# A hybrid streaming encoder step on one core: regrouped retention products, sample tile padded to 128, tables and warm-up products moved

## The chip, the core and the metric

The kernel is one launch on one NeuronCore of a Trainium2 chip. The metric is the device time of one execution in microseconds (us), the median of several runs; beside it stands one profiled execution, whose trace is read below. The engines are TensorE (PE in the profile: matrix products into PSUM banks, with its weight loads as PEld), VectorE (DVE), ScalarE (ACT), GpSimd (POOL) and SyncE (SP, which here only issues DMAs). A DMA can be issued by POOL's queue as well.

## What is computed

One inference step of a two-layer trunk for 512 prompt tokens and 64 sample tokens, width 1024, all in float32. Layer 0 runs an mLSTM (4 heads of 128) and a multi-scale retention (4 heads, keys 64, values 128) side by side from one input projection; layer 1 is a latent attention (MLA, 8 heads) with a block-causal mask of chunks of 64. A SwiGLU FFN follows each, and a layer norm follows each part. The three recurrent parts that the change touches, cut from the reference:

```python
# retention, chunk by chunk
a = jnp.einsum('bhtd,bhsd->bhts', qc, kc) * intra
o = jnp.einsum('bhts,bhsv->bhtv', a, vc) + q_dec[..., None] * jnp.einsum('bhtd,bhdv->bhtv', qc, S)
S_new = s_dec[:, None, None] * S + jnp.einsum('bhsd,bhsv->bhdv', kc * k_dec[..., None], vc)
...
# mLSTM, chunk by chunk (stabilised gates in d_mat, m_t, w_inter, w_k, decay)
s = jnp.einsum('bhtd,bhsd->bhts', qc, kc) * jnp.exp(d_mat - m_t[..., None])
num = w_inter[..., None] * jnp.einsum('bhvd,bhtd->bhtv', C, qc) + jnp.einsum('bhts,bhsv->bhtv', s, vc)
C_new = decay[..., None, None] * C + jnp.einsum('bhsv,bhsd->bhvd', vc * w_k[..., None], kc)
...
# MLA, per block of queries
p = jax.nn.softmax(jnp.where(vis, s, -jnp.inf), axis=-1)
return jnp.einsum('bqhk,bkhv->bqhv', p, v)
```

## The kernel before

Tokens stand in five tiles: tile 0 is the 64 sample tokens, tiles 1 to 4 are 128 prompt tokens each. All weights stream from memory in blocks of 512 KB into three raw buffers (`raw0` to `raw2`), issued by SP in the order of their use; each half of a block is split into a high part (a rounding by ACT, line 364) and a low part (a subtraction by DVE, line 362), and a product is three products high x high, high x low, low x high. A product on TensorE is the helper `mm` (line 465), a transpose the helper `transpose` (line 533). An f32 product shows as two records in the trace.

The order of every engine's instructions is fixed when the program is written: the code runs the projections unit by unit, and after each unit a small planner (`tick`) lets background tasks go on whose due time has come on its own clock. Retention, mLSTM and attention are such tasks, so their small products lie between the k steps of the projections. What stands on an engine's queue is worked off in that order, and an instruction that waits holds all behind it. PSUM has eight banks in three pools, each used in a ring: `mm` with three (projections), `x` with four (small products), `o` with one (only used in layer 1 before the change).

At the start, SP brings the input (first half of each row, in pieces) and the weights by turns. POOL's own queue brings the small tables: at lines 587 to 590 the gate weights `wg`, the `rope`, `mask`, `cst` and `ident` tables and the gate bias `bif`; at lines 640 to 649 the selection tables, the initial states `c0` (into `CxS`) and `s0` (into `S[0]`) and the norm vectors. The first projection `rqrk` loops over k, and for each k over tiles 1 and 2, since the weights only just arrive; its second half of the input comes inside the loop, after k = 3 and k = 4. Then come `gate_mm`, `rqrk` for tiles 0, 3 and 4, and `rv` and `mv`. Every `rqrk` tile goes through `ev_qk`: three DVE ops read the bank (lines 706 to 708), three POOL ops add and scale (709, 711, 713), and then TensorE transposes the result into `qkT`.

`retention` has three steps per tile. `s1` makes the four heads' scores, k and q of 64 rows each, in two x banks, and DVE applies the mask into `P` (line 925). `s2` computes for each head in turn the state's increment `up` (64 columns of weights), P times v (128 rows) and q times the state (64 rows); then DVE adds `up` to the state and scales it (lines 944, 947) and does the head norm from the banks (lines 952 to 958). `s3` transposes the result. `mlstm` has the same for one head at a time: `s1` a transpose and two products, `s2` P v, the state's increment and q C; tile 0 has 64 rows in all of these. In layer 1 `sa`, `sb` and `sc` are the scores, the transposes of the probabilities and the product with v; for tile 0 `sc` is nine products of 64 columns into the o bank. `wgp`, `T0`, `T1`, `Z`, `r7` and the like are names of long-lived buffers in SBUF.

Of the kernel before, what the change touches and what calls it, by code (L numbers as in the profile page):

```python
# [8 lines left out]
F32 = mybir.dt.float32  # L9
# [208 lines left out]
class Kern:  # L218
# [335 lines left out]
    def setup(self):  # L554
# [24 lines left out]
        wg = self.T0[:, 4300:4364]  # L579
# [43 lines left out]
    def layer0(self):  # L623
# [16 lines left out]
        nc.gpsimd.dma_start(self.sel, t["sel"])  # L640
        nc.gpsimd.dma_start(self.reset, t["reset"])
        nc.gpsimd.dma_start(self.m0, t["m0"])
        self.CxS = r6[:, 1413:1929].rearrange("p (h c) -> p h c", h=4)
        self.CxP = Z[:, 3456:3972].rearrange("p (h c) -> p h c", h=4)
        nc.gpsimd.dma_start(self.CxS, t["c0"])
        self.S = (T1[:, 4032:4288].rearrange("p (a v) -> p a v", a=2), Z[:, 3584:3840].rearrange("p (a v) -> p a v", a=2))
        nc.gpsimd.dma_start(self.S[0], t["s0"])
        nc.gpsimd.dma_start(self.gv, t["gv"])
        nc.gpsimd.dma_start(self.lnv, t["lnv"])
        nc.gpsimd.tensor_scalar(self.gv, self.gv, 0.5, None, ALU.mult)  # L650
# [41 lines left out]
        def ev_qk(i, ps):  # L692
            L = TLEN[i]
            V, G = nc.vector, nc.gpsimd
# [14 lines left out]
            G.tensor_tensor(t1, t1, t2, ALU.add)  # L709
            gam = self.cst[0:L, 0:8].unsqueeze(2)  # L710
            G.tensor_tensor(t1[:, 0:4, :], t1[:, 0:4, :], gam[:, 0:4, :].to_broadcast([L, 4, 64]), ALU.mult)
            kt = self.ktok[0:L, i, :].rearrange("p (h d) -> p h d", h=4)
            G.tensor_tensor(kt, t1[:, 4:8, :], gam[:, 4:8, :].to_broadcast([L, 4, 64]), ALU.mult)
# [33 lines left out]
        for k in range(KT):  # L747
# [7 lines left out]
            for i in (1, 2):  # L755
                self.tm(banks[i][0:TLEN[i], :], "rqrk", [k], self.xt(i), first=k == 0, last=k == KT - 1)
                if k == KT - 1:
                    ev_qk(i, banks[i])
            if k in (3, 4):
                j = k - 3  # L760
                nc.sync.dma_start(half_view(Z, 1, 4 * j, 4 * j + 4), half_dram(t["x"], 1, 4 * j, 4 * j + 4))
        gate_mm(0)
# [12 lines left out]
        nc.gpsimd.memset(mvb[:, :, :, 128:129], 1.0)  # L775
        tm_units("mv", ev_mv)
# [134 lines left out]
    def retention(self):  # L911
# [16 lines left out]
        def s2(i):  # L928
# [3 lines left out]
            up = banks[1][:, 256:512]  # L932
            for h in range(4):
                a, p0 = h // 2, 64 * (h % 2)
                oh = banks[h % 2][0:L, a * 128:(a + 1) * 128]
                vh = self.rv[:, i, h * 128:(h + 1) * 128]
# [4 lines left out]
            O = lambda h: banks[h % 2][0:L, (h // 2) * 128:(h // 2) * 128 + 128]  # L941
            up3 = up.rearrange("p (a v) -> p a v", a=2)
            if i != 1:
                V.tensor_tensor(st, st, up3, ALU.add)
            for a in range(2):
                c = 8 + 2 * (i == 0) + a
                V.tensor_scalar(st[:, a, :], st[:, a, :] if i != 1 else up3[:, a, :], self.cst[:, c:c + 1], None, ALU.mult)
# [13 lines left out]
        def s3(i):  # L961
            L, s = TLEN[i], TSTART[i]
            x = self.xbank()
# [5 lines left out]
        nc.gpsimd.memset(P[0][64:128, :, 0:64], 0.0)  # L969
# [49 lines left out]
    def mlstm(self, h, done):  # L1019
# [9 lines left out]
        def s1(i):  # L1029
            L, s = TLEN[i], TSTART[i]  # L1030
            x = self.xbank()
            self.transpose(x[0:L, 0:128], kT[:, s:s + L])
# [1214 lines left out]
```

## Time and profile before

| | us |
|---|---|
| median of 3 runs (1407.14 to 1411.38) | 1410.47 |
| profiled execution | 1404.45 |
| its span, first to last instruction | 1402.7 |
| TensorE busy in the span | 1364.9 (97%) |
| VectorE busy | 969.1 (69%) |
| ScalarE busy | 612.1 (44%) |
| GpSimd busy | 172.1 (12%) |
| mean DMA flow over the span | 81 GB/s |

The busy share of an engine says how much of the span it has something in work; matrix products are pipelined, so a busy TensorE need not be at its peak. The chain of waits follows the end of the run back, at each step to what released the instruction. A timeline row is one group of like instructions with its start, its time and, in brackets, the idle time ahead of it and what ended that. A row of windows gives, for one stretch, its length, the busy time (and number of instructions) of PE, PEld, DVE, ACT and POOL, TensorE's granted clock, the busy share of the 16 DMA engines and their GB/s; a DMA queue's row gives packets, MB and the time of its packets as a share of the 16 engines' time. Line numbers are those of the kernel before.

### The profile page before, as it was taken

What the parts mean: (1) busy time and instruction counts of PE and PEld (TensorE: products, weight loads), DVE (VectorE), ACT (ScalarE), POOL (GpSimd) and SP (SyncE); (2) the same over time, 40 slices, a digit from 0 to 9 for tenths busy, and PEclk for the clock granted to TensorE, in tenths of its full rate; (3) what the DMA queues carried; (4) which work ended last, traced back from release to release, by engine and by line L of the source; (5) the groups of instructions that cost most, each with busy time, mean ns of one, the idle gap of its engine ahead of it and who ended that gap; (6) DMA issues with size and microseconds to landing.
All of it is one profiled execution on the core that took longest, in us unless ns stands there. A gap on an engine that the chain in (4) does not pass through costs nothing.

```text
span 1402.7 us, 24691 instructions
## 1 busy us (share of the span) xinstructions
PE 1364.9 (97%) x9787; PEld 1307.0 (93%) x9787; DVE 969.1 (69%) x2252; ACT 612.1 (44%) x1295; POOL 172.1 (12%) x207
## 2 busy tenths in 40 slices
PE   7999999999999999999999999999999999999995
PEld 5777999998999999999988899999899999999995
DVE  5655677767973586478898665567797358647877
ACT  4422333435552354255445465543555235425533
POOL 5300010104200000000021433311320000000000
PEclk9999999999999999999999999999999999999997
DMA  6111121521233122222422100021222312222222
GB/s 216 61 61 38 61 61 61 182 67 61 76 98 114 61 91 91 91 76 92 135 78 73 38 31 31 31 91 39 83 76 97 115 61 91 91 91 76 91 76 68
DMA packets 37315, 112.92 MB, mean 81 GB/s; under 512 B 4504, under 2 KB 11608, under 8 KB 37200
## 3 DMA queue, kind: packets, MB, share of 16 engines
q1 hardware_dynamic: 36656, 110.33, 23.4%
q8 instruction: 77, 1.26, 0.4%
q0 software_dynamic: 544, 1.02, 0.2%
q14 instruction: 38, 0.31, 0.1%
HBM read 107.45 MB, written 3.89 MB: 79 GB/s over the span
## 4 chain that ended last, share of the span: by engine, by line
PE 85%; DVE 9%; ACT 2%; DMA 1%; issue 1%; POOL 1%; SPq 0%; POOLq 0%; ACTq 0%; DVEq 0%
PE mm L465 45%; PE x L465 37%; PE x L533 2%; DVE r L362 2%; DVE Z L1266 1%; DVE Z L1252 1%; DMA raw<-in_w 1%; PE o L465 1%; ACT Xh L1298 1%; ACT Z L1305 0%; DMA Z<-in_x 0%; ACT r L364 0%; DVE small L541 0%; DVE small L543 0%; DVE small L542 0%
## 5 line engine op out<-in xcount | busy, mean ns | idle before, releaser
L465 PE MATMUL mm<-H,r 128*128 128x320 f32 (+2 forms) x2832 | 386.3, 296 | 0.0
L465 PEld LDWEIGHTS mm<-H,r 128*128 128x128 f32 x2832 | 377.2, 188 | 0.4
L465 PE MATMUL x<-Xh,r 128*128 128x288 f32 x1216 | 244.7, 295 | 0.0
L465 PE MATMUL mm<-Xh,r 128*128 128x288 f32 (+2 forms) x1152 | 232.2, 300 | 6.0 <-DVE Z L1172 2.9
L364 ACT CAST r<-raw 128x512 fp32r<-128x512 f32 (+2 forms) x292 | 178.6, 648 | 109.0 <-PE mm L465 78.3
L362 DVE TENSOR_TENSOR r<-raw,r 128x512 fp32r<-128x512 f32 (+2 forms) x276 | 196.1, 740 | 40.1 <-ACT r L364 36.7
L465 PE MATMUL x<-r,r 128*128 128x288 f32 (+3 forms) x1534 | 212.5, 293 | 0.2 <-DVE r L1042 0.2
L465 PEld LDWEIGHTS x<-r,r 128*128 128x128 f32 (+1 forms) x1534 | 205.7, 188 | 1.7 <-issue 0.7
L465 PEld LDWEIGHTS x<-Xh,r 128*128 128x128 f32 x1216 | 194.5, 188 | 0.5
L465 PEld LDWEIGHTS mm<-Xh,r 128*128 128x128 f32 x1152 | 186.3, 192 | 7.2 <-ACT Z L1305 3.8
L465 PE MATMUL x<-Xl,r 128*128 128x288 f32 x608 | 179.2, 295 | 0.0
L465 PE MATMUL mm<-Xl,r 128*128 128x288 f32 (+2 forms) x576 | 167.8, 299 | 0.0
L364 ACT CAST r<-T 128x512 fp32r<-128x512 f32 (+1 forms) x114 | 87.0, 763 | 127.1 <-DVE T L397 114.8
L465 PEld LDWEIGHTS x<-Xl,r 128*128 128x128 f32 x608 | 114.0, 188 | 0.0
L362 DVE TENSOR_TENSOR r<-T,r 128x512 fp32r<-128x512 f32 (+1 forms) x114 | 96.3, 866 | 18.0 <-ACT r L364 18.0
L465 PEld LDWEIGHTS mm<-Xl,r 128*128 128x128 f32 x576 | 108.2, 191 | 0.1
L465 PE MATMUL mm<-r,Xh 128*128 128x512 f32 (+1 forms) x320 | 99.1, 392 | 6.6 <-ACT r L364 4.8
L1306 POOL TENSOR_TENSOR Xl<-Z,Xh 128x288 fp32r<-128x288 f32 (+2 forms) x36 | 31.0, 861 | 467.6 <-ACT Z L1305 467.1
L465 PEld LDWEIGHTS mm<-r,Xh 128*128 128x128 f32 x320 | 58.7, 191 | 20.2 <-ACT r L364 5.6
L1210 ACT ACTIVATE T<-Z 128x288 f32<-128x288 f32 (+2 forms) x56 | 24.9, 445 | 91.8 <-DVE Z L1172 47.4
L465 PE MATMUL mm<-r,Xl 128*128 128x512 f32 (+1 forms) x160 | 61.3, 383 | 0.0
L1567 DVE TENSOR_TENSOR T<-T,x 128x288 f32<-128x288 f32 x38 | 17.2, 454 | 60.3 <-PE x L465 60.3
(316 smaller groups left out, 1732.8 us busy)
## 6 DMA issues: line engine op xcount, KB each, us to landing
raw<-in_w SPq DMA_DIRECT2D x169, 512.0 KB, 3.5
r<-in_w SPq DMA_DIRECT2D x20, 512.0 KB, 3.6
Z<-in_x SPq DMA_DIRECT2D x1, 1280.0 KB
o_y<-Z SPq DMA_DIRECT2D x2, 640.0 KB, 3.2
Z<-in_x SPq DMA_DIRECT2D x2, 512.0 KB, 5.8
Z<-in_x SPq DMA_DIRECT2D x1, 1024.0 KB, 9.0
o_y<-Z SPq DMA_DIRECT2D x4, 256.0 KB, 2.2
Z<-in_x SPq DMA_DIRECT2D x3, 320.0 KB, 9.1
```

The costliest lines, as they stand in the source:

```text
L362: self.lo_engine.tensor_tensor(t[:, 1], src, t[:, 0].bitcast(F32), ALU.subtract)
L364: self.nc.scalar.copy(t[:, 0], src)
L465: self.nc.tensor.matmul(out, lhsT, rhs, start=start, stop=stop, skip_group_check=more)
L533: self.nc.tensor.transpose(out, in_, self.ident[0:n, 0:n])
L1210: nc.scalar.activation(q, z, AF.Square)
L1252: V.tensor_tensor(z, z, xd[:, 0:n], ALU.subtract)
L1266: V.scalar_tensor_tensor(z, z, gain(m), R[:, 0:n], ALU.mult, ALU.mult)
L1298: A.activation(self.Xh[:, a:b], z, AF.Identity, bias=bias(m))
L1306: G.tensor_tensor(self.Xl[:, a:b], z, self.Xh[:, a:b].bitcast(F32), ALU.subtract)
L1567: V.tensor_tensor(s[:, 0:n], s[:, 0:n], ps, ALU.add)
```

## The change

The tables come by SP's queue: `rope`, `ident`, `mask`, `cst`, `wg`, `bif` after k = 3 of the `rqrk` loop, ahead of the second half of the input, and the seven others after the loop. Eight products of `ones` by `ones` into the o bank stand ahead of everything on TensorE. In `ev_qk` the three POOL ops go to DVE. Retention's `s1` takes all 128 columns and uses the o bank and an mm bank; `s2` runs all increments first, two heads in one product of 128 by 256, of which the diagonal blocks are used, then all P v, then all q S; the state update is one product by the decay and four multiply-adds of 64 rows; `s3` uses an mm bank. mLSTM's tile 0 uses 128 rows and columns, with the rows beyond 64 set to zero by POOL. In layer 1 the probabilities of tile 0 are transposed as 128 rows, over a part of `T0` that POOL clears once; `sc(0)` takes high and low probabilities as one operand of 128 columns for the high part of v and another product of 64 columns for the low part, and ACT and DVE add the two halves. In the diff, blank parts and lines that only follow from this are left out.

```diff
-        nc.gpsimd.dma_start(wg, t["wg"])
-        for name in ("rope", "mask", "cst", "ident"):
-            nc.gpsimd.dma_start(getattr(self, name), t[name])
-        nc.gpsimd.dma_start(self.bif, t["b_if"].to_broadcast([128, 8]))
+        x = self.obank()
+        for _ in range(8):
+            self.mm(x[:, 0:128], self.ones, self.ones, True, True)
...
-        nc.gpsimd.dma_start(self.sel, t["sel"])
...
-            G.tensor_tensor(t1, t1, t2, ALU.add)
+            V.tensor_tensor(t1, t1, t2, ALU.add)
...
+            if k == 3:
+                for name in ("rope", "ident", "mask", "cst"):
+                    nc.sync.dma_start(getattr(self, name), t[name])
+                nc.sync.dma_start(T0[:, 4300:4364], t["wg"])
+                nc.sync.dma_start(self.bif, t["b_if"].to_broadcast([128, 8]))
             if k in (3, 4):
...
+        for dst, name in ((self.sel, "sel"), (self.reset, "reset"), (self.m0, "m0"), (self.CxS, "c0"), (self.S[0], "s0"),
+                          (self.gv, "gv"), (self.lnv, "lnv")):
+            nc.sync.dma_start(dst, t[name])
...
         def s1(i):
-            for o in range(2):
-                x3 = self.xbank()[:, 0:256].rearrange("p (a t) -> p a t", a=2)
+            for o, bank in enumerate((self.obank(), self.bank())):
+                x3 = bank[:, 0:256].rearrange("p (a t) -> p a t", a=2)
                 p0 = 64 * o
                 for a in range(2):
-                    self.mm(x3[0:L, a, 0:L], self.qkT[p0:p0 + 64, 2 + a, s:s + L], self.qkT[p0:p0 + 64, a, s:s + L], True, True)
+                    self.mm(x3[:, a, :], self.qkT[p0:p0 + 64, 2 + a, s:s + 128], self.qkT[p0:p0 + 64, a, s:s + 128], True, True)
...
         def s2(i):
+            for a in range(2):
+                self.mm(banks[a][:, 256:512], self.ktok[:, i, a * 128:(a + 1) * 128], self.rv[:, i, a * 256:(a + 1) * 256],
+                        True, True)
             for h in range(4):
-                self.mm(up[p0:p0 + 64, a * 128:(a + 1) * 128], self.ktok[:, i, h * 64:(h + 1) * 64], vh, True, True)
-                self.mm(oh, P[i % 2][:, h, 0:L], vh, True, i == 1)
-                if i != 1:
-                    self.mm(oh, self.qkT[p0:p0 + 64, a, s:s + L], st[p0:p0 + 64, a, :], False, True)
+                self.mm(oh[h], P[i % 2][:, h, :], self.rv[:, i, h * 128:(h + 1) * 128], False, i == 1, more=True)
             if i != 1:
-                V.tensor_tensor(st, st, up3, ALU.add)
+                for h in range(4):
+                    a, p0 = h // 2, 64 * (h % 2)
+                    self.mm(oh[h], self.qkT[p0:p0 + 64, a, s:s + 128], st[p0:p0 + 64, a, :], False, True, more=True)
+                V.tensor_tensor(st, st, self.cst[:, c:c + 2].unsqueeze(2).to_broadcast([128, 2, 128]), ALU.mult)
...
+                        V.scalar_tensor_tensor(to, up, dec, to, ALU.mult, ALU.add)
...
         def s3(i):
-            x = self.xbank()
+            x = self.bank()
...
-            self.mm(x[0:L, 128:128 + L], kT[:, s:s + L], qT[:, s:s + L], True, True)
+            self.mm(x[:, 128:256], kT[:, s:s + 128], qT[:, s:s + 128], True, True)
...
-            self.mm(x[0:L, 0:129], Ps[i], v[0:L, i, :], True, True)
+            self.mm(x[:, 0:129], Ps[i], v[:, i, :], True, True)
...
+        G.memset(T0[:, 2560:4096], 0.0)
...
                 if i == 0:
-                    groups = [(0, 64, 0, (0, 1, 2), 0)]
+                    x2 = x[:, 0:128].rearrange("p (b q) -> p b q", b=2)
+                    for j in range(3):
+                        vh, vl = vt[0][:, j, vc:vc + 128], vt[1][:, j, vc:vc + 128]
+                        self.mm(x2, vh, pt0[:, :, j, :], j == 0, False)
+                        self.mm(x[:, 64:128], vl, pt0[:, 0, j, :], False, j == 2)
+                    tmp = self.smalls(64)
+                    A.copy(tmp, x[:, 0:64])
+                    V.tensor_tensor(x[:, 64:128], x[:, 64:128], tmp, ALU.add)
+                    return
```

Where this stands in the engines' orders. On SP, at the start, from the fourth weight block on (`raw0` again), before; `Z<-in_x` is the second half of the input:

```order
L342 DMA raw0_27_127<-in_w 128x1024
L342 DMA raw1_29_150<-in_w 128x1024
L761 DMA Z_1_69<-in_x 128x4x256
L342 DMA raw2_31_176<-in_w 128x1024
L761 DMA Z_1_69<-in_x 128x4x256
L342 DMA raw0_33_200<-in_w 128x1024
```

The same on SP after the change:

```order
L342 DMA raw0_28_122<-in_w 128x1024
L342 DMA raw1_30_145<-in_w 128x1024
L752 DMA rope_14_82<-in_rope 128x640
L752 DMA ident_8_76<-in_ident 128x128
L752 DMA mask_13_81<-in_mask 128x256
L752 DMA cst_15_83<-in_cst 128x12
L753 DMA T0_2_70<-in_wg 128x64
L754 DMA bif_16_84<-in_b_if 128x8
L757 DMA Z_1_69<-in_x 128x4x256
L342 DMA raw2_32_177<-in_w 128x1024
L757 DMA Z_1_69<-in_x 128x4x256
L342 DMA raw0_34_201<-in_w 128x1024
```

Six tables now stand between two weight blocks and the second half of the input, and the second half stands behind them.

On TensorE, `s1` of tiles 0 and 1 within the `mv` product of tile 0 (`mm_64`), and the start of the next tile's product (`mm_72`), before; the first number of a bank's name counts the banks handed out:

```order
L465 MATMUL x_67_683<-Z_1_69 64x64 x2
L465 MATMUL x_68_687<-Z_1_69 64x64 x2
L465 MATMUL x_69_691<-Z_1_69 128x128 x2
L465 MATMUL x_70_695<-Z_1_69 128x128 x2
L465 MATMUL mm_64_662<-r0_26_122,H_6_74 128x512 x4
L465 MATMUL mm_64_662<-r1_28_145,H_6_74 128x512 x4
L465 MATMUL mm_72_714<-r3_32_195,Xh_4_72 128x512 x2
```

The same on TensorE after:

```order
L465 MATMUL o_68_696<-Z_1_69 128x128 x2
L465 MATMUL mm_69_697<-Z_1_69 128x128 x2
L465 MATMUL o_70_704<-Z_1_69 128x128 x2
L465 MATMUL mm_71_705<-Z_1_69 128x128 x2
L465 MATMUL mm_65_675<-r0_27_117,H_6_74 128x512 x4
L465 MATMUL mm_65_675<-r1_29_140,H_6_74 128x512 x4
L465 MATMUL mm_73_727<-r3_33_196,Xh_4_72 128x512 x2
```

Both tiles' scores now lie in the o bank and in mm banks, and the next `mv` product follows them in the ring of three mm banks (65, 69, 71, 73).

On TensorE, `s2` of tile 2, the first two heads of four, before (`T1` holds v, `Z` keys, queries and the state, `r4` the masked scores):

```order
L465 MATMUL x_84_860<-T1_3_71,Z_1_69 64x128
L465 MATMUL x_83_859<-T1_3_71,r4_23_109 128x128
L465 MATMUL x_83_859<-Z_1_69 128x128
L465 MATMUL x_84_860<-T1_3_71,Z_1_69 64x128
L465 MATMUL x_84_860<-T1_3_71,r4_23_109 128x128
L465 MATMUL x_84_860<-Z_1_69 128x128
```

All four heads of the same step after:

```order
L465 MATMUL x_84_872<-T1_3_71,Z_1_69 128x256
L465 MATMUL x_85_873<-T1_3_71,Z_1_69 128x256
L465 MATMUL x_84_872<-T1_3_71,r4_24_112 128x128
L465 MATMUL x_85_873<-T1_3_71,r4_24_112 128x128
L465 MATMUL x_84_872<-T1_3_71,r4_24_112 128x128
L465 MATMUL x_85_873<-T1_3_71,r4_24_112 128x128
L465 MATMUL x_84_872<-Z_1_69 128x128
L465 MATMUL x_85_873<-Z_1_69 128x128
L465 MATMUL x_84_872<-Z_1_69 128x128
L465 MATMUL x_85_873<-Z_1_69 128x128
```

The products of one kind now stand side by side.

## Rows read from the trace of the kernel before

**Rows 1.** The page, part 4: the chain's shares of the span, by engine.

```profile
PE 85%; DVE 9%; ACT 2%; DMA 1%; issue 1%; POOL 1%; SPq 0%; POOLq 0%; ACTq 0%; DVEq 0%
```

**Rows 2.** TensorE's waits, whole run: us in total, times, longest us.

```profile
PE x L533 <- DVE r L958: 1.4, 1, 1.4
```

**Rows 3.** Timeline of TensorE, start: start us, us, what, [idle before <-releaser].

```profile
4.83 1.52 PE L465 MATMUL mm<-r,Xh 128*128 128x512 f32 x2 [4.83 <-ACT r L364]
...
20.89 0.30 PE L465 MATMUL x<-Xh,wgp 128*16 128x320 f32 x1
21.03 0.30 PE L465 MATMUL x<-Xl,wgp 128*16 128x320 f32 x1
...
31.45 0.33 PE L533 MATMUL x<-ident,r 128*128 128x128 f32 x1 [1.10 <-POOL r L711]
32.20 0.33 PE L533 MATMUL x<-ident,Z 128*128 128x128 f32 x1 [0.42 <-POOL Z L713]
```

**Rows 4.** Windows of all engines, 10 to 20 us; DMA queues, 0 to 30 us.

```profile
10.00:20.00 10.00, 9.99 (x38) 7.22 (x37) 6.97 (x14) 6.19 (x15) 3.32 (x7) 1.00 1.03 375
...
q0 software_dynamic: 544, 1.02, 9.5%
```

**Rows 5.** Timeline of VectorE, rope work of the first stage.

```profile
25.14 0.69 DVE L706 TENSOR_TENSOR r<-mm,rope 128x512 f32<-128x512 f32 x1
...
26.41 0.68 DVE L706 TENSOR_TENSOR r<-mm,rope 128x512 f32<-128x512 f32 x1
...
47.68 4.42 DVE L362 TENSOR_TENSOR r<-raw,r 128x512 fp32r<-128x512 f32 x4
```

**Rows 6.** Timeline of TensorE, retention's s2 of tiles 0, 1 and 3.

```profile
83.89 0.43 PE L465 MATMUL x<-T,Z 128*64 128x128 f32 x2
...
87.23 0.72 PE L465 MATMUL x<-Z 64*128 64x128 f32 x8
...
92.01 0.43 PE L465 MATMUL x<-T,Z 128*64 128x128 f32 x2 [1.07 <-DVE r L958]
...
95.15 0.72 PE L465 MATMUL x<-Z 64*128 64x128 f32 x8
...
112.22 0.43 PE L465 MATMUL x<-T,Z 128*64 128x128 f32 x2
...
117.00 0.73 PE L465 MATMUL mm<-r,Xh 128*128 128x512 f32 x2
```

**Rows 7.** Timeline of TensorE, f32 products of full shape in a layer norm.

```profile
725.33 0.68 PE L465 MATMUL x<-T,ones 128*128 128x256 f32 x2
725.84 0.50 PE L465 MATMUL x<-cvec,T 128*128 128x2 f32 x4
...
735.40 0.60 PE L465 MATMUL x<-T,ones 128*128 128x128 f32 x4
```

**Rows 8.** Timelines of TensorE and VectorE around s1 and the head norm.

```profile
79.03 2.13 PE L465 MATMUL mm<-r,H 128*128 128x512 f32 x8
...
79.79 1.13 DVE L925 TENSOR_TENSOR r<-x,mask 64x128 f32<-64x128 f32 x4
...
82.41 0.27 DVE L740 TENSOR_TENSOR r<-mm,Z 64x128 f32<-64x128 f32 x1
87.33 0.42 DVE L944 TENSOR_TENSOR T<-T,x 128x256 f32<-128x256 f32 x1 [4.65 <-PE x L465]
...
92.20 0.74 DVE L925 TENSOR_TENSOR r<-x,mask 128x256 f32<-128x256 f32 x2
```

**Rows 9.** Timeline of TensorE, mLSTM's s2 of tile 0, first head.

```profile
149.89 0.85 PE L465 MATMUL x<-r,r 64*64 64x129 f32 x4
...
151.03 0.33 PE L533 MATMUL x<-ident,Z 128*128 128x128 f32 x1
```

**Rows 10.** Timeline of TensorE, MLA's sc of tile 0, first head.

```profile
807.12 1.17 PE L465 MATMUL o<-r,r 128*128 128x64 f32 x9
808.13 1.84 PE L465 MATMUL mm<-H,r 128*128 128x320 f32 x12
```

More of the change, by code (lines that the diff above doesn't have):

```diff
@@ L775, in layer0 @@
         nc.gpsimd.memset(mvb[:, :, :, 128:129], 1.0)
+        for x in (mva[64:128, 0], mvb[64:128, 0], r7[64:128, 1290:1418], r6[:, 1029:1157]):
+            nc.gpsimd.memset(x, 0.0)
         tm_units("mv", ev_mv)
@@ L941, in s2 @@
-            O = lambda h: banks[h % 2][0:L, (h // 2) * 128:(h // 2) * 128 + 128]
-            up3 = up.rearrange("p (a v) -> p a v", a=2)
-            if i != 1:
-                V.tensor_tensor(st, st, up3, ALU.add)
-            for a in range(2):
-                c = 8 + 2 * (i == 0) + a
-                V.tensor_scalar(st[:, a, :], st[:, a, :] if i != 1 else up3[:, a, :], self.cst[:, c:c + 1], None, ALU.mult)
+            O = lambda h: banks[h % 2][0:L, (h // 2) * 128:(h // 2) * 128 + 128]
+            oh = [banks[h % 2][:, (h // 2) * 128:(h // 2) * 128 + 128] for h in range(4)]
@@ new lines, in s2 @@
+            c = 8 + 2 * (i == 0)
+            if i != 1:
+                V.tensor_tensor(st, st, self.cst[:, c:c + 2].unsqueeze(2).to_broadcast([128, 2, 128]), ALU.mult)
+            for a in range(2):
+                for p0 in (0, 64):
+                    up = banks[a][p0:p0 + 64, 256 + 2 * p0:384 + 2 * p0]
+                    dec = self.cst[p0:p0 + 64, c + a:c + a + 1]
+                    to = st[p0:p0 + 64, a, :]
+                    if i == 1:
+                        V.tensor_scalar(to, up, dec, None, ALU.mult)
+                    else:
+                        V.scalar_tensor_tensor(to, up, dec, to, ALU.mult, ALU.add)
@@ L1860, in layer1 @@
         qrt = [T1r[:, 3136 + 576 * j:3712 + 576 * j] for j in range(2)]
-        for a in [pt0[64:128, p, 2] for p in range(2)] + [t[64:128, 2] for t in vt]:
-            G.memset(a.bitcast(F32), 0.0)
+        for a in vt:
+            G.memset(a[64:128, 2].bitcast(F32), 0.0)
+        G.memset(T0[:, 2560:4096], 0.0)
         mask = H[:, 8768:8960]
@@ L2004, in sc @@
                 if i == 0:
-                    groups = [(0, 64, 0, (0, 1, 2), 0)]
-                else:
-                    c0 = TSTART[i - 1] - 320 * half
-                    groups = [(c0, 256, 0, tuple(range(3, 2 + i)), 0), (c0 + 128, 128, 128, (2 + i,), i - 1)]
-                full = [pt0[:, 0], pt0[:, 1]]
-                if i:
-                    full = [x.rearrange("p (j q) -> p j q", q=256) for x in (ptA if i < 3 else ptB)]
+                    x2 = x[:, 0:128].rearrange("p (b q) -> p b q", b=2)
[7 more added lines that the diff above has]
+                    return
+                c0 = 0 if half else 128
+                groups = [(c0, 256, 0, tuple(range(3, 2 + i)), 0), (c0 + 128, 128, 128, (2 + i,), i - 1)]
+                full = [x.rearrange("p (j q) -> p j q", q=256) for x in (ptA if i < 3 else ptB)]
                 for gi, (c, n, q0, ts, j0) in enumerate(groups):
@@ L2024, in sc @@
                     a, b = hcols(half, h)
-                    split(self.Xh[:, a:b], self.Xl[:, a:b], x[:, 0:b - a])
+                    c = 64 * (1 - half)
+                    split(self.Xh[:, a:b], self.Xl[:, a:b], x[:, c:c + b - a])
             def task(i):
```

47 lines of the change are left out of this document (16 added, 31 removed).

## The prediction

> **What bounds the kernel now.** I read the chain of waits first: it runs 85% of the span through TensorE [rows 1], so a change counts by what it takes from TensorE's own time, by a wait of TensorE that it ends, or by one that it makes. Then TensorE's list of waits: most of them lie at layer norms and FFNs that the change doesn't touch; those within its reach are the two on the head-norm writes of line 958, one of 1.4 us [rows 2] and one in retention's rows below, and at the start the 4.83 us before the first product and the 1.10 and 0.42 us on POOL's rope work (lines 711, 713) [rows 3]. Last the timeline of the stages that the edits rewrite, for what their small products cost: there TensorE is busy all the time, but with products of changing shape that take several times what products of one shape take.
>
> **The start (tables, warm-up, rope ops).** Two ends set the start. TensorE's: the k loop over the arriving weight blocks ends at 20.89, where the gate products begin; it is followed by these, tile 0 and the transposes of tiles 1 and 2, of which the last pair begins at 32.20, behind POOL [rows 3]. From 10 to 20 us the DMA engines are full (share 1.03, 375 GB/s), and the POOL queue moves 1.02 MB in the first 30 us beside the weights [rows 4]. In the order printed above, the rope, ident, mask, cst and wg tables (by their shapes 0.55 MB) go behind the fourth and fifth weight block, and the state tables (0.4 MB) behind the seventh. 0.55 MB at 375 GB/s is 1.5 us, all 1.02 MB would be 2.7; the second weight block comes 1.5 to 2.3 sooner by this, and the end of the k loop with it, 18.6 to 19.4. The second end is DVE's. Its chain for tiles 1 and 2 starts at 25.14, when the last half of x is split, and one tile's three rope ops keep it until 26.41, 1.27 us [rows 5]; the three moved ones have the same shapes and I give them the same 1.27. Tile 1 and tile 2 thus end at 25.14 + 4 x 1.27 = 30.2. The last half of x now has 0.4 MB less ahead of it, 1.1 us, so 29.1; the last transpose pair would then begin at about 29.2 and not 32.20. TensorE's side (11.3 us less the 1.5 of waits after the loop's end) gives 28.4 to 29.2. I take -3.0 us; bounds 0 (the transfers come no sooner, or SP's own waits give it back) and -4.5 (TensorE's side alone). In this order SP waits for each DMA's place in a ring of eight: the first half-x DMA waits for the landing of the fourth weight block, the next weight block for the fifth; behind them stand all later weights. These weights are on their way before the tables, so I price this wait at nothing beyond the 1.1; if it holds, it shows as the bound of 0.
>
> The 8 warm-up products (16 records) end before the first weight is split at 4.83 and cost nothing as long as they take under 4 us; if they took longer, the first products wait behind them, and those have slack up to the second block. What they may give is the clock: the first two records take 1.52 us [rows 3]. But these first products are followed by waits for the second block, so that only what TensorE has left to do once that block is there can gain, under 1 us; taken as 0.
>
> After 32 us tiles 0, 3 and 4 put three more ops on DVE, 1.27 each. Against that, DVE loses time now when POOL works: four low parts of weights (line 362) take 4.42 us at 47.68 beside POOL's rope work [rows 5], where four are 2.7 by the 0.69 of an equal shape (line 706, [rows 5]); that is 1.7 back. Net -0.3, bounds -1.0 and +0.7.
>
> **Retention.** Tile 0's s2 runs from 83.89 to 87.23, 3.34 us; tile 1's from 92.01 to 95.15, 3.14; tile 3's from 112.22 to 117.00, 4.78, and tiles 2 and 4 are like it [rows 6]. After, s2 is two products of 256 columns, 0.51 us for one by the distance of the rows at 725.33 and 725.84; four of 128 columns, 0.22 each: four records show 0.60 in all, 0.11 each if the last shows 0.27 [rows 7]; and four of 64 rows in alternating halves, 8 records, for which the 8 of s1, 0.72 with the tail, give 0.65 [rows 6]. Together 1.0 + 0.9 + 0.65 = 2.5, and 1.9 in tile 1, which has no state. So 0.8 + 1.2 + 3 x 2.3 = 8.9 us less. s1 keeps its count of products. The trace already shows that shape changes cost: 4.78 us for 24 records is 0.20 each against 0.11.
>
> A rule speaks against the regrouping: the Trainium skill, "TensorE: Matmul & The Clock Gate", Part 3 (Packing small matmuls), says that products that leave half of the array idle should be packed side by side, because they then overlap. By it the two 64-column halves could share a time, so that padding throws away up to half of two products, some 0.5 us a tile and 2.5 in all; the rows of tile 0 (3.34 us for 24 records, 0.14 each) show no gain over 0.11, so the sum goes without it.
>
> The two waits on line 958 go, 1.4 us [rows 2] and 1.07 at 92.01 [rows 6], -2.5: they come from the ring of four x banks, which s1 and s3 no longer use. In their place stand waits on one o bank and three mm banks. (1) s1(1) needs the o bank of s1(0), that is the mask of s1(0) on DVE. DVE begins the four masks at 79.79 (1.13 for four, so the first ends at 80.07), behind low parts of weights; TensorE has all of s1(0) and s1(1) done at 79.03 [rows 8]. With 0.5 for s1(1) it would be done at 80.6, so +1.6. Queued behind it is the rest of mv tile 0. (2) The mv product of tile 1 takes the bank that mv tile 0 leaves, in the ring of three 65, 69, 71, 73 in the printed order. It was free before; now it waits until lines 527, 739 and 740 have emptied it. The last of them starts at 82.41 and ends at 82.68, and the eight products ahead, 2.13 us from 79.03, end at 81.0 to 81.16 [rows 8]: +1.6. (3) s1(3) on the o bank waits for the mask of s1(2), which stands on DVE behind tile 0's state and head norm, 87.33 to 92.20 and its own 0.37 [rows 8], 5.2 us, and 0.6 more since the state update gets five ops for three. TensorE has s1(2) 0.65, four k steps (at most 92.01 - 1.07 - 87.88 = 3.1; I take 2.8) and s2(1) 1.9 in between, 5.35; so +0.5, and with the second bank's mask (0.37) and the copy of line 743 some +1.2. (4) From tile 2 on, DVE's 6.5 us a tile lie beside a whole mv product of eight k steps; +0.4. New waits 4.8, bounds 2 and 8. The stage: -8.9 - 2.5 + 4.8 = -6.6, bounds -9.5 and -3.
>
> **mLSTM.** s2(0) takes 149.89 to 151.03, 1.14 us [rows 9], in three products of two shapes; with 128 rows and columns 6 x 0.11 = 0.66. s1(0)'s change of shape I put at 0.17 (bounds 0 and 0.3). Times four heads: -2.6, bounds -1.2 and -3.6. The extra POOL memsets stand far ahead.
>
> **MLA.** sc(0) is nine records of 64 columns in 1.01 us, 0.112 each, from 807.12 to 808.13 [rows 10]; six instead save 0.34 a head, 2.7 in eight (three of the six have 128 columns; of this kind 64 columns take 0.112 and 320 columns 0.14, from 20.89 to 21.03 [rows 3], so 0.12 at most). The transposes of 128 rows save a change of shape, 0 to 0.27 each time, I take 0.15, 1.2. The ACT copy and DVE add a head stand for a cast and a subtract that go. The memset of T0 on POOL costs 0 to 1 once. -3.9, bounds -5 and -2.
>
> **Sum.** -3.0 - 0.3 - 6.6 - 2.6 - 3.9 = -16.4 us. The profiled execution took 1404.45, 1402.7 of it span, and lies 6.0 under the median of 1410.47; I carry the difference over: 1388.1 profiled, 1394 median.
>
> **Rivals.** (a) The start gains nothing: w0 and w1 come by the same queue in the same order, and what TensorE gets sooner it waits for later. For it: the POOL queue's share is 9.5% of the DMA time in the first 30 us [rows 4]. Against it: the queue is full exactly where TensorE waits. 1394 + 3 = 1397. (b) The bank waits repeat for every tile: each s1 waits for the whole DVE chain of the tile ahead, and each mv product for the bank before it, 3 x 1.6 + 2 x 1.2 = 7.2 more, 1401. For it: DVE's 6.5 us against 5.4 of TensorE at tile 0. Against it: from tile 2 on a whole mv product (5.6 us) lies between. (c) The padding loses overlap: if two halves of 64 columns did share their time, half of two products of 0.51 is lost in each of five tiles, 2.5 us, and as much again in mLSTM and MLA at most: 1399. The rule named above speaks for it, tile 0's 0.14 a record against it. (d) Slower: the tables in SP's queue. SP waits in order, so a table's late landing holds every later weight. If the six tables and two halves of x land one after another and not side by side, at 3.5 us for each (an estimate; the first block with its split took 4.83 [rows 3]), six make 21 us, the -3.0 becomes +18, and the time 1415. It decides once SP stands still for over 19 us before the sixth weight block. Against it: only the landings of weights that were due anyway are waited for.
>
> **How the numbers follow.** Forecast 0.70, (a) 0.12, (b) 0.09, (c) 0.05, (d) 0.04. The bounds add to -23.6 and -5.5: 1387 to 1405. The range 1386 to 1405 holds the forecast and most of (a) to (c). A measurement of this kernel tells a change from none at about 0.3%, 4.2 us. Faster: the forecast, (a), (c) and most of (b), less what a second bad cause could add, 0.91; same 0.05; slower 0.04.
>
> **What would show it.** In the profile after: the last transposes of tile 2 near 29; TensorE's s2 at 2.5 us a tile; no waits on the head-norm line; instead waits on the masks near s1(1) and s1(3) and on line 731's bank, 4 to 5 us together; sc(0) at 0.67. Wrong would be: SP idle before the sixth block, a wait at each of five tiles, or s2 above 3.5.

## The result and the profile after

The changed kernel takes 1393.31 us (median of 4 runs, 1392.03 to 1393.74) against 1408.81 for the kernel before in the same series (1403.07 to 1411.38); the ratio is 0.9894 with a 95% interval of 0.9861 to 0.9927. The forecast was 1394, within 1386 to 1405. The profiled execution took 1393.54 us, 1391.6 of it span, 11.1 less than the profiled span before; the forecast for it was 1388.1, 16.4 less. So the median is hit and the sum of the terms is not: retention gained more than forecast, mLSTM somewhat less, the start little, and the attention stage lost.

TensorE's waits in the whole run, those that are new and the ones that belong to the stages of the change (columns as in [rows 2]):

```profile
PE o L465 <- DVE o L2022: 3.9, 5, 1.1
...
PE o L465 <- DVE r L928: 2.7, 2, 1.4
PE mm L465 <- DVE r L699: 2.6, 1, 2.6
...
PE x L533 <- DVE r L1070: 1.0, 1, 1.0
```

The 1.4 us wait on the head norm of [rows 2] is gone; of that line, 970 now, one wait of 0.3 us is left. The longest in sum, 3.9 us on line 2022, is one that the forecast doesn't have: that line is the DVE add in `sc(0)`. Line 928 is retention's mask, line 699 the last of a rope tile's ops that read a projection's bank.

**The start.** TensorE, start us, us, what, idle before, to set beside [rows 3]:

```profile
4.84 1.52 PE L465 MATMUL mm<-r,Xh 128*128 128x512 f32 x2
...
18.97 0.31 PE L465 MATMUL x<-Xh,wgp 128*16 128x320 f32 x1
...
27.82 1.20 PE L465 MATMUL mm<-r,Xh 128*128 128x512 f32 x2 [2.61 <-DVE r L699]
28.81 0.63 PE L465 MATMUL mm<-r,Xl 128*128 128x512 f32 x1
...
32.76 0.27 PE L533 MATMUL x<-ident,r 128*128 128x128 f32 x1
```

The warm-up products end before 4.84, and the k loop ends at 18.97 and not 20.89, as forecast. But then the product of tile 3 waits 2.61 us for the bank of tile 1, its records run at half the clock (two in 0.99 us, from 27.82 to 28.81), and the last transposes begin at 32.76, not at 29.2. The product after them started at 32.51 before and starts at 32.90 now. DVE's rows say why, beside [rows 5]:

```profile
23.67 1.43 DVE L601 TENSOR_TENSOR Xl<-Z,Xh 128x256 fp32r<-128x256 f32 x4 [1.30 <-ACT Xh L600]
25.11 1.30 DVE L362 TENSOR_TENSOR r<-raw,r 128x512 fp32r<-128x512 f32 x2
26.33 0.69 DVE L697 TENSOR_TENSOR r<-mm,rope 128x512 f32<-128x512 f32 x1
...
27.26 0.42 DVE L699 TENSOR_TENSOR r<-mm,rope 128x256 f32<-128x256 f32 x1
27.71 0.69 DVE L700 TENSOR_TENSOR r<-r 128x512 f32<-128x512 f32 x1
```

The low parts of the last half of the input begin at 23.67. In the kernel before they began at 22.49:

```profile
22.49 1.43 DVE L602 TENSOR_TENSOR Xl<-Z,Xh 128x256 fp32r<-128x256 f32 x4 [1.32 <-ACT Xh L601]
23.94 1.29 DVE L362 TENSOR_TENSOR r<-raw,r 128x512 fp32r<-128x512 f32 x2
```

In this execution that half came 1.2 us later and not 1.1 sooner; so line 699 ends at 27.7, and TensorE, which is there earlier, waits for it. What held it stands in the chain of waits (start, us, what), first after and then before:

```profile
11.66 4.33 DMA rope<-in_rope
...
16.00 7.21 DMA Z<-in_x
```

```profile
15.94 6.09 DMA Z<-in_x
```

SP could issue the second part of the half only when the rope table, issued at 11.66, had landed. It left at 16.00, no sooner than before (15.94), though the weight block ahead of the half left sooner, at 11.28 for 13.09, and it took 7.21 us to land for 6.09.

**Retention.** TensorE in the same stretch as [rows 6]:

```profile
76.10 2.03 PE L465 MATMUL mm<-r,H 128*128 128x512 f32 x8
...
80.18 0.37 PE L465 MATMUL o<-Z 64*128 64x128 f32 x1 [1.40 <-DVE r L928]
...
82.79 0.63 PE L465 MATMUL mm<-r,Xh 128*128 128x512 f32 x2
...
85.58 1.02 PE L465 MATMUL x<-T,Z 128*128 128x256 f32 x4
...
87.98 0.27 PE L465 MATMUL o<-Z 64*128 64x128 f32 x1
...
94.72 0.37 PE L465 MATMUL o<-Z 64*128 64x128 f32 x1 [1.28 <-DVE r L928]
...
108.03 1.03 PE L465 MATMUL x<-T,Z 128*128 128x256 f32 x4
...
110.53 0.73 PE L465 MATMUL mm<-r,Xh 128*128 128x512 f32 x2
...
123.95 0.54 PE L465 MATMUL mm<-Xh,r 128*128 128x320 f32 x2
```

Tile 0's s2 takes 85.58 to 87.98, 2.40 us, and tile 3's 108.03 to 110.53, 2.50, where 2.5 was forecast. s1(1) waits 1.40 us at 80.18 and s1(3) 1.28 at 94.72, both for a mask. The mv product of tile 1 follows at 82.79 without any wait. The stage, from the eight products before s1 to the first product of the next projection, takes 76.10 to 123.95, 47.85 us. In the kernel before it took 76.04 to 132.09, 56.05 us, so it is 8.2 us shorter:

```profile
76.04 2.02 PE L465 MATMUL mm<-r,H 128*128 128x512 f32 x8
...
132.09 0.54 PE L465 MATMUL mm<-Xh,r 128*128 128x320 f32 x2
```

**mLSTM**, beside [rows 9]:

```profile
141.53 0.61 PE L465 MATMUL x<-r,r 128*128 128x129 f32 x4
...
142.20 0.27 PE L533 MATMUL x<-ident,Z 128*128 128x128 f32 x1
...
165.48 0.61 PE L533 MATMUL x<-ident,r 64*128 64x64 f32 x3 [1.02 <-DVE r L1070]
```

s2 of tile 0 takes 0.67 us (141.53 to 142.20), 0.66 in the forecast. In the second head a wait of 1.02 us on the state's write on DVE (line 1070) has come up, where the kernel before lost 0.2.

**MLA**, beside [rows 10]:

```profile
795.76 0.75 PE L465 MATMUL o<-r,r 128*128 128x128 f32 x6
796.44 0.86 PE L533 MATMUL x<-ident,T 64*128 64x64 f32 x5
798.44 1.16 PE L465 MATMUL o<-raw,r 128*128 128x256 f32 x6 [1.14 <-DVE o L2022]
```

sc(0) takes 0.68 us for six records (795.76 to 796.44), 0.67 in the forecast. Then, at 798.44, the products of sc(2) wait 1.14 us. They write other columns of the same o bank. DVE in that stretch:

```profile
797.16 0.16 DVE L1983 RECIPROCAL small<-small 128x1 f32<-128x1 f32 x1 [0.90 <-ACT T L1981]
797.43 0.49 DVE L1984 TENSOR_SCALAR T<-T,small 128x512 f32<-128x512 f32 x1
797.83 0.42 DVE L1902 SCALAR_TENSOR_TENSOR T<-mm,T 128x256 fp32r<-128x256 f32 x1
798.16 0.22 DVE L2022 TENSOR_TENSOR o<-o,small 128x64 f32<-128x64 f32 x1
```

The add that TensorE waits for takes 0.22 us, but it stands in DVE's queue behind a reciprocal that itself waited 0.90 us for ACT's exponential, behind a softmax scale and a part of the next head's keys, and runs at 798.16, 1.7 us after sc(0). The copy on ACT that it needs stands behind the same exponential and runs at 797.29.

Not all of the profiles' 11.1 us is the change's. In the layer norm near 990 us, which the change doesn't touch, the clock stood at half for a while in the profile before and not in this one (rows of windows, first before, then after: length, PE busy, clock, DMA):

```profile
985.00:1003.00 18.00, 15.26 (x90) 0.81 0.47 147
```

```profile
970.00:990.00 20.00, 16.65 (x122) 1.00 0.51 159
```

That stretch of before lies 8 to 11 us earlier in the run after, and accounts for 3 of the 11.1 us: from the row of before at 991.68 (983.46 after) to that at 1001.53 (990.18) the distance between the two kernels grows from 8.22 to 11.35 us. The profile after has stretches of half clock of its own, one at the start and one in the attention stage (clock 0.71 from 800 to 804 us); a second profile of the same kernel, below, has neither, and its attention stage is 1.6 us shorter. The times of several runs are the measure, and the experiments below.

### The profile page after: what moved, and what is told of

Same layout as the page of the kernel before. It is cut to its first block, busy times and chain, and to the rows that moved or that the text cites. A ratio compares the mean times of both kernels' runs of the same rounds, so it can differ in the third digit from the quotient of the medians.

```text
span 1391.6 us, 24628 instructions
## 1 busy us (share of the span) xinstructions
PE 1351.7 (97%) x9759; PEld 1305.6 (94%) x9759; DVE 979.5 (70%) x2277; ACT 610.8 (44%) x1295; POOL 155.0 (11%) x182
## 4 chain that ended last, share of the span: by engine, by line
PE 83%; DVE 10%; ACT 3%; DMA 2%; issue 2%; POOL 0%; SPq 0%; POOLq 0%; ACTq 0%; DVEq 0%
PE mm L465 44%; PE x L465 36%; PE x L533 2%; DVE r L362 2%; DVE Z L1279 1%; DMA raw<-in_w 1%; DVE Z L1265 1%; PE o L465 1%; ACT Xh L1311 1%; DMA Z<-in_x 1%; ACT r L364 0%; ACT Z L1318 0%; DVE small L542 0%; DVE small L541 0%; DVE small L543 0%
## 5 line engine op out<-in xcount | busy, mean ns | idle before, releaser
L465 PE MATMUL mm<-Xh,r 128*128 128x288 f32 (+2 forms) x1152 | 229.2, 297 | 6.4 <-DVE Z L1185 2.8
L465 PE MATMUL x<-r,r 128*128 128x288 f32 (+2 forms) x1534 | 211.7, 293 | 0.2 <-DVE r L1055 0.2
L465 PEld LDWEIGHTS x<-r,r 128*128 128x128 f32 x1534 | 205.9, 188 | 0.5 <-DVE r L1055 0.5
L465 PEld LDWEIGHTS mm<-Xh,r 128*128 128x128 f32 x1152 | 183.4, 189 | 7.7 <-ACT Z L1318 3.8
L362 DVE TENSOR_TENSOR r<-T,r 128x512 fp32r<-128x512 f32 (+1 forms) x114 | 96.3, 866 | 18.6 <-ACT r L364 18.6
```

The costliest lines, as they stand in the source:

```text
L362: self.lo_engine.tensor_tensor(t[:, 1], src, t[:, 0].bitcast(F32), ALU.subtract)
L465: self.nc.tensor.matmul(out, lhsT, rhs, start=start, stop=stop, skip_group_check=more)
```

## The experiments

Each kernel is the changed one with one edit, unless it says otherwise. They ran in three series, each on one chip beside the kernel before.

| run | median us | runs | ratio to the kernel before (95%) |
|---|---|---|---|
| a0_after | 1393.5 | 6 | 0.9906 (0.9885 to 0.9927) |
| e1_add_late | 1389.46 | 6 | 0.9880 (0.9858 to 0.9902) |
| e2_mla_before | 1390.58 | 6 | 0.9886 (0.9865 to 0.9907) |
| e4_tables_late | 1392.08 | 6 | 0.9898 (0.9877 to 0.9919) |
| e3_start_before | 1393.02 | 5 | 0.9916 (0.9902 to 0.9931) |
| e5_ret_before | 1402.41 | 12 | 0.9984 (0.9969 to 1.0000) |
| e6_mlstm_before | 1395.48 | 5 | 0.9931 (0.9918 to 0.9944) |
| e7_rope_pool | 1395.38 | 5 | 0.9933 (0.9920 to 0.9946) |
| e8_no_warm | 1392.82 | 6 | 0.9916 (0.9901 to 0.9930) |
| e9_two_mends | 1387.09 | 4 | 0.9875 (0.9857 to 0.9892) |
| e10_three_mends | 1384.03 | 4 | 0.9850 (0.9832 to 0.9869) |
| e11_ret_only | 1394.48 | 6 | 0.9929 (0.9913 to 0.9945) |

The kernel before had medians of 1406.16, 1405.02 and 1404.07 us in the three series (the first four rows, the next four, the last four). The changed kernel stands in the first of them only, so what is set against its 1393.5 us from the other two is compared across chips, and there a difference of less than about 2 us is not certain.

**The changed kernel again.**

> The changed kernel once more, as the measure for the three below on the same chip. Both theories: 1393 us (1391 to 1396), and a span in which the same four stages stand as in its first trace: the start even with the kernel before, retention about 8 us shorter, the mLSTM stage 2 to 3 us shorter, the attention stage about 2 us longer.

1393.5 us, and its profile shows the same waits. Two things differ, and matter for reading the start. The last half of the input reaches DVE at 22.59, 0.1 us later than in the kernel before and not 1.2:

```profile
22.59 1.43 DVE L601 TENSOR_TENSOR Xl<-Z,Xh 128x256 fp32r<-128x256 f32 x4 [2.31 <-ACT Xh L600]
```

And the granted clock differs. Windows of the two profiled executions, 20 to 32 us, first the one above, then this (length; PE, PEld, DVE, ACT, POOL busy; clock; DMA share; GB/s):

```profile
20.00:32.00 12.00, 9.39 (x39) 7.11 (x37) 9.62 (x23) 4.59 (x12) 0.00 (x0) 0.86 0.56 180
```

```profile
20.00:32.00 12.00, 9.33 (x45) 7.02 (x43) 9.51 (x21) 4.31 (x10) 0.00 (x0) 1.00 0.46 149
```

The wait on line 699 is there in both, 2.6 and 2.3 us, but only in the first does the clock fall behind it. The product that follows the transposes starts at 32.90 in the first and at 31.26 here, where the kernel before had 32.51. So the start is even with the kernel before in one execution and 1.3 us shorter in the other.

**The late add.**

```diff
-                    tmp = self.smalls(64)
-                    A.copy(tmp, x[:, 0:64])
-                    V.tensor_tensor(x[:, 64:128], x[:, 64:128], tmp, ALU.add)
                     return
...
+                if i == 2:
+                    tmp = self.smalls(64)
+                    A.copy(tmp, x[:, 0:64])
+                    V.tensor_tensor(x[:, 64:128], x[:, 64:128], tmp, ALU.add)
                 if i in (2, 4):
```

> Only the ACT copy and the DVE add of sc(0) move: they stand after the products of sc(2), just ahead of the split. Theory A (the attention stage lost its gain to TensorE waiting for that add before sc(2) may write into the same bank): the five waits of 3.9 us on the add go, the stage ends 3 to 4 us sooner, the time is 1389 to 1390.5. Rival B (the attention stage is longer for another reason: the planner's changed order of products, or the six products cost as much as the nine): the waits move to the split or to the next head's bank, and the time stays within 1 us of the changed kernel.

1389.46 us, 4.0 less. TensorE in the same place of the first head:

```profile
795.24 0.75 PE L465 MATMUL o<-r,r 128*128 128x128 f32 x6
795.92 0.86 PE L533 MATMUL x<-ident,T 64*128 64x64 f32 x5
796.54 0.89 PE L465 MATMUL o<-raw,r 128*128 128x256 f32 x6
```

sc(2) follows its transposes at once (796.54); the five waits are gone from the list, and none of their size has come in the stage. Theory A holds.

**The attention stage as before.** All its edits undone.

> All edits of the attention stage undone, the others kept. Theory A (the stage costs 2 us net with its edits): 1391 (1390 to 1392). The forecast's own sum (the edits bring 3.9 us): 1397. Rival B as for the run with the late add: 1391 too, but then the late add changes nothing.

1390.58 us: the kernel is 2.9 us faster without the stage's edits, where the forecast had it 3.9 slower. Against the late add, 1389.46, the stage's edits are worth 1.1 us in the medians once the wait is away, within the scatter of these runs (1388.69 to 1392.98 here). The traces tell it apart better. From the transposes that wait for the norm of line 1733 to the first product that waits for line 1185 behind the stage, TensorE takes 185.09 us with the stage as before (741.16 to 926.25, and the same 185.09 in the kernel before), 186.80 in the second profile of the changed kernel (740.50 to 927.30) and 182.65 with the late add (739.99 to 922.64). So at full clock the edits cost 1.7 us as they were made and bring 2.4 with the late add.

**The tables behind the input.**

```diff
             if k == 3:
-                for name in ("rope", "ident", "mask", "cst"):
-                    nc.sync.dma_start(getattr(self, name), t[name])
                 nc.sync.dma_start(T0[:, 4300:4364], t["wg"])
-                nc.sync.dma_start(self.bif, t["b_if"].to_broadcast([128, 8]))
             if k in (3, 4):
...
+            if k == 4:
+                for name in ("rope", "cst", "ident", "mask"):
+                    nc.sync.dma_start(getattr(self, name), t[name])
+                nc.sync.dma_start(self.bif, t["b_if"].to_broadcast([128, 8]))
```

> The gate weights stay where the change puts them, the rope, cst, ident, mask and bias tables go behind the second half of the input in SP's queue. Theory C (the tables ahead of the second half of the input made it land 1.2 us later, DVE's rope chain later by the same, TensorE wait 2.6 us for the bank of tile 1 and run at half its clock for 3 us after that): the last half lands 1 to 2 us sooner, the wait is under 1 us, the records after it 233 ns apart, and the time 2 to 4 us shorter, 1389.5 to 1391.5. Rival D (DVE's chain with the three rope ops sets the end whatever lands when): the wait stays over 2 us and the time within 1 us of the changed kernel.

The second part of the last half leaves SP at 14.41 and not at 16.00. DVE is done with the input at 22.81, where it was at 25.11 in the first trace and at 24.04 in the second, and TensorE goes from tile 0's products into tile 3's without a stop (21.65 + 3.90 us, next at 25.51):

```profile
22.81 1.29 DVE L362 TENSOR_TENSOR r<-raw,r 128x512 fp32r<-128x512 f32 x2
```

```profile
21.65 3.90 PE L465 MATMUL mm<-r,H 128*128 128x512 f32 x16
25.51 0.70 PE L465 MATMUL mm<-r,Xh 128*128 128x512 f32 x2
...
30.03 0.72 PE L465 MATMUL mm<-r,Xh 128*128 128x512 f32 x2
```

The product that followed the transposes at 32.90 starts at 30.03. The time, 1392.08, is 1.4 us less than the changed kernel's, less than the 2 to 4 that C expected, and by itself hardly above what the runs scatter. In the traces the product is 2.9 us earlier than in the first profile and 1.2 earlier than in the second. That the wait is gone speaks for C and against D; C's size was too high, since it took the first profile, with its late input and its half clock, for the rule.

**The start's transfers as before.** Tables on POOL's queue, no warm-up, rope ops still on DVE.

> The 13 tables go back to POOL's queue and the warm-up products are left out; the rope ops stay on DVE. Theory C (the move makes the second half of the input land later and gives back what the second weight block gains): the k loop ends at 20.9 again, the last transposes of tile 2 begin near 30, and the time is 1392 to 1395, the same as the changed kernel's 1393.4. The forecast's step (the move alone brings 2 to 3 us): 1395.5 to 1396.5.

1393.02 us, the same as the changed kernel within what can be told across chips. Its k loop ends at 20.34, and its transposes of tile 2 end at 30.8, with no wait on the bank and no fall of the clock. So the move of the tables, as it was made, brings nothing that can be measured, though it brings the k loop's end forward; the rope ops on DVE alone can carry what the start gains.

**The rope ops on POOL again.**

> The three rope ops of each tile on POOL again, all other edits kept. Theory (the move to DVE brings the transposes of tile 2 forward by about 1.5 us at the start, and after 32 us its cost and its gain cancel): the waits on POOL of 1.1 and 0.4 us are back and the time is 1394.5 to 1396. Rival (DVE is the later end either way): 1393 to 1394.

1395.38 us, 1.9 more than the changed kernel across chips, and 2.4 more than the run above in its own series; as expected, but not by the waits expected: the two on POOL don't appear, since in its profile the wait on line 699 (2.6 us) and a stretch of half clock come first and hide them. The next product starts at 33.86. What POOL's ops cost by themselves at full clock is therefore not shown.

**No warm-up.**

> The changed kernel without its eight warm-up products. Theory (they raise the clock for the first records, but the start ends with DVE's rope chain): the first records of the k loop are 427 ns apart for longer, the loop ends 0.5 to 1.5 us later, and the time stays within 1 us of the changed kernel, 1392.5 to 1394.5. Rival (the warm-up is what brings the loop's end forward and the end of the start with it): 1395 or more.

1392.82 us, across chips. The warm-up brings nothing that can be measured. It does not bring the loop's end forward either, against what was expected here: the end is at 18.7 without it, 18.97 and 18.3 with it.

**Retention as before.**

> Retention as before (s1, s2, s3, their banks and the state update), all other edits kept. Theory (the first trace puts 8 us on this stage): 1401 to 1402. The forecast's sum: 1400. Rival (the new bank waits eat the gain and the time comes from elsewhere): under 1397. Its two waits on the head norm and s2 of 4.8 us a tile are back.

1402.41 us, 9 more than the changed kernel, so retention is the larger part of the whole gain. The 12 executions fall into two groups, 7 of 1400.6 to 1402.5 us at a mean granted clock of 0.991 to 0.992, and 5 of 1405.2 to 1407.1 at 0.987 to 0.989. The profiled one is of the second, and its windows show where (length; PE, PEld, DVE, ACT, POOL busy; clock; DMA):

```profile
107.00:113.00 6.00, 4.64 (x23) 3.16 (x23) 4.76 (x24) 0.59 (x1) 0.00 (x0) 1.00 0.00 0
113.00:121.00 8.00, 8.00 (x23) 5.38 (x24) 1.93 (x11) 0.00 (x0) 0.00 (x0) 0.51 0.00 0
```

```profile
111.14 0.66 PE L533 MATMUL x<-ident,r 128*128 128x128 f32 x4 [1.36 <-DVE r L961]
...
112.09 0.49 PE L465 MATMUL x<-T,r 128*128 128x128 f32 x2
...
115.41 0.80 PE L465 MATMUL x<-T,r 128*128 128x128 f32 x2
...
118.93 1.22 PE L465 MATMUL mm<-r,Xh 128*128 128x512 f32 x2
```

Behind the 1.36 us wait on the head norm, during the s2 of changing shapes, the clock goes to 0.51, half of full speed: a pair of records of 128 by 128 that takes 0.49 us at full clock (112.09) takes 0.80 (115.41), and the weights' products after it (118.93) start at half clock too. In the profiled kernel before, the same stretch is at full clock:

```profile
113.00:121.00 8.00, 7.86 (x39) 1.00 0.00 0
```

From the first product of tile 3's s2 to the next transposes TensorE takes 12.13 us in this profile (111.73 to 123.86) and 7.67 in the kernel before (112.22 to 119.89), 4.5 us more, which is the distance of the two groups. That the other four executions of the slower group lost their time at the same place is not shown; each has no profile. The 7 of the faster group have a median of 1401.87, 8.4 us above the changed kernel.

**Retention alone.** The kernel before with the retention edits only.

> The kernel before with the retention edits alone. Theory (8 us of TensorE and waits, and a stretch of half clock behind the 1.4 us wait that the old retention has in some runs and the new one in none): 1395.5 to 1398, and no run above 1400, where the kernel before spreads from 1401 to 1411. Rival (the spread of the kernel before comes from elsewhere, such as the POOL queue's tables): the same mean gain of 8 us, but a spread of 8 us as before.

1394.48 us, 9.6 less than the kernel before in the same series, and 1392.5 to 1396.9 in six executions, none above 1400. About the spread it settles little: 4.4 us in six executions, where the kernel before spread 5.8 in eleven in this series, and its profile, one of the slower ones, has the clock at 0.83 in the first 20 us. Against the rival, by which the tables on POOL's queue cause the spread, stand two other runs: with the old retention and the tables on SP it is 6.6 us, with the new retention and the tables on POOL (the start's transfers as before) 3.2. Nor is the new retention free of the fall: in the profile with the attention stage as before the clock falls behind its 1.40 us wait on the mask, and the eight products after it take 3.23 us (79.39 to 82.62) and not 1.96.

**mLSTM as before.**

> mLSTM's tile 0 with 64 rows and columns again, all other edits kept. Theory (the traces put 2 to 2.5 us on it, of which 1.0 is given back to a wait on the state's write on DVE in one head): 1395.5. The forecast: 1396. Rival (the padding brings nothing here): 1393.4, and s2 of tile 0 as long as after.

1395.48 us, 2.0 to 2.2 more than the changed kernel across chips: as expected.

**Two mends, and three.** The late add and the late tables together; then also x banks for s1 of tiles 1 and 3:

```diff
-            for o, bank in enumerate((self.obank(), self.bank())):
+            for o, bank in enumerate((self.xbank(), self.xbank()) if i % 2 else (self.obank(), self.bank())):
```

> The late add of sc(0) and the tables behind the second half of the input together. If both gains stand by themselves (3.9 and 1.4 us of the medians so far): 1387 to 1388.5. If they overlap: 1389.5.

> The two mends, and s1 of tiles 1 and 3 in x banks again, tiles 0, 2 and 4 as the change has it. Theory (s1(1) waits 1.4 us only for the one o bank; the x banks are free at that point): that wait goes, s1(3) waits about 1 us for the head norm of tile 0 and not 1.3 for the mask, and the time is 1.3 to 2 us below the kernel with two mends, 1385.5 to 1387. Rival (the ring of four x banks passes the wait on to s2, as before the change): within 0.5 us of the two mends.

1387.09 us, as expected if both gains stand by themselves, and 1384.03: 9.3 us below the changed kernel across chips, 8.8 below the run without the warm-up in the same series, and the fastest of all. The waits on the mask are gone from TensorE's list; what is left at s1(3) is one of 0.70 us:

```profile
89.47 1.04 PE L465 MATMUL x<-Z 64*128 64x128 f32 x8 [0.70 <-PE x L465]
```

It beats what was expected of it (1.3 to 2 us under the two mends) by a microsecond, with four executions of each; the waits account for 2.0 us of its 3.1 (1.40, and 1.28 less 0.70), the rest is not explained.

## Why the prediction was right, and where its steps failed

The time is right, 1393.3 for 1394, and that it is so close is luck: two errors cancel. The sum took 16.4 us off the profiled execution, 1404.45, to 1388.1; the profiled execution after took 1393.54, 10.9 less, so the sum was 5.5 too high. But the forecast also carried over the 6.0 us by which the median before lay above its profile, and after the change the median lies 0.2 below it. In the three later series, with 11 to 17 executions of the kernel before, its median is 1404.07 to 1406.16 and not 1410.47. What holds up is the mechanism of the largest term, retention; the start and the attention stage were wrong.

- **Retention, forecast -6.6, measured -8.2 in the traces and -8.9 to -9.6 in the times.** The price of s2 by rows of one shape is right to 0.1 us a tile (2.40 and 2.50 for 2.5), and the two waits on the head norm went, but for 0.25 us at 122.92. The waits that took their place were sized too high, 2.7 us for 4.8: 1.40 and 1.28 for 1.6 and 1.2, but step (2), 1.6 us for the mv product's bank, did not come at all. The ring of three was read off as a strict turn (65, 69, 71, 73), by which the product had to wait until tile 0's mv bank was empty. It started at 82.79, before the copy of line 527 (83.05) or line 730 (83.73) had even begun on that bank, so it had another, one of the two score banks, whose masks ended at 80.3 and 81.7; which of them, no row shows. What the traces leave over to the times is, as far as one profile shows, the half clock behind the old wait, which the forecast could not see, as the profiled execution before did not have it: against the faster group of the run with the old retention the gain is 8.4.
- **The start, forecast -3.0, measured between +0.4 and -1.3.** The step that failed is "the last half of x now has 0.4 MB less ahead of it, 1.1 us". Fewer bytes lay ahead, but SP's queue issues in turn: the six issues and their waits stand before that half. Its first part left SP at 14.51 instead of 13.46, and its second, on which the chain hangs, waited for the rope table's landing and left at 16.00, where it had left at 15.94 without the tables. It came 1.2 us later in the first profile and 0.1 in the second. The text had named this wait, SP's place in the ring, and set it at nothing. TensorE's own side, the loop's end at 18.6 to 19.4, was right at 18.97 and was worth nothing, since it then waits for DVE. This is rival (a), by which TensorE waits later for what it gets sooner, with SP's wait as the cause; with the tables behind the input the second part leaves at 14.41, and the start stands at -2.5 in that profile.
- **32 to 76 us, forecast -0.3:** the product at 32.90 stood 0.4 behind the kernel before, the one at 76.10 stands 0.06 behind, so -0.3.
- **mLSTM, forecast -2.6, measured -2.0 to -2.2.** The size of s2 is right; the wait of 1.02 us on the state's write takes a part back. In the traces the distance between the two kernels grows by 2.3 us from the end of retention (132.09 and 123.95) to the layer norm behind mLSTM (298.43 and 287.99).
- **MLA, forecast -3.9, measured +2.9 in the times and +1.7 in the trace at full clock.** The products of sc(0) cost what was forecast. The step that failed is "the ACT copy and DVE add a head stand for a cast and a subtract that go". As busy time they do; but the cast and subtract were off TensorE's path, and the add writes the bank into which TensorE's next products go. A step was priced by its duration, 0.22 us, where what counts is its place in DVE's queue and who is queued behind it. The late add shows it: same work, 4.0 us less. With it the stage brings 2.4 us in the trace, still 1.5 short of the 3.9; the 1.2 us for the transposes were a choice between 0 and 0.27 each, and no run tests them alone.
- **Padding.** The rule on packing small products, Part 3 of "TensorE: Matmul & The Clock Gate" in the Trainium skill, was set against the sum. Its price, 0.5 us a tile, did not appear: the padded s2 of tile 0 takes 2.40 us where its form in halves, in changing order, took 3.34 [rows 6]. But that form did not pack the halves side by side, and no run does, so the rule itself is not tested here. Where two halves do run side by side, in s1, they start 0.01 us apart (o and mm banks at 78.06 and 78.07), as the rule has it; the change kept that.
- **Slower (rival d):** SP stood still as named, but its waits for landings in the first 40 us add to 2.7 us, the longest 1.4, not to nineteen; in the kernel before they added to 3.9.

## What to carry over

Group small products by shape and price them by a row of one shape. Of every instruction put between two groups of products, ask not how long it takes but what its queue holds ahead of it and whether TensorE's next write goes to the same bank; if so, move it behind that write. A table put ahead of the data that the critical engine needs delays it by the queue's order, even where bytes are saved: put it behind. And a median that lies off its profile is not a constant to carry over: ask first what spreads the executions, and whether the change removes it.

## What was not expected of the hardware

TensorE's granted clock fell to half, 1.2 for 2.4 GHz, for some 3 to 10 us behind waits of 1.4 to 2.6 us, in some executions and not in others: at 113 to 123 us in the profile with the old retention (0.51) and not in the profiled kernel before, at 27.8 us in one profile of the changed kernel and not in the other, and behind the mask's wait of 1.40 us in the profile with the attention stage as before. With the old retention the executions fell into two groups some 4.5 us apart, and the one profile of the slower group loses as much in that stretch. What sets the moment of the fall was not tried.
